# Layer norms of a two-layer hybrid decoder step: squares summed over features before the products, a short token block taken as a full one

## The chip, the cores and the metric

The kernel runs on one core of a Trainium2 chip. Its metric is the device time of one execution in microseconds (us), and the median of the runs counts. The engines are named as in the profile: PE is TensorE's matmul and PEld its weight loads, DVE is VectorE, ACT is ScalarE, POOL is GpSimd, SP issues most DMAs.

## What is computed

A prompt of 1024 tokens and 8 sample rows of 4 tokens go through two layers, together 1056 tokens of 1024 features. Each layer ends its two halves with a layer norm over the features:

```python
def layer_norm(x, g, b):
    xf = x.astype(jnp.float32)
    mu = jnp.mean(xf, -1, keepdims=True)
    var = jnp.mean(jnp.square(xf - mu), -1, keepdims=True)
    return ((xf - mu) * lax.rsqrt(var + LN_EPS)).astype(x.dtype) * g + b
...
    x = layer_norm(ALPHA * x + mix @ P['w_out'], P['ln1_g'], P['ln1_b'])
    h = jnp.square(jax.nn.relu(x @ P['w_ff_up']))
    x = layer_norm(ALPHA * x + h @ P['w_ff_down'], P['ln2_g'], P['ln2_b'])
```

The rest (RWKV-7 time mixing, windowed attention, gates) is untouched and is not told here.

## The kernel before

Activations lie feature-major: 8 feature tiles of 128 partitions, the tokens along the free dimension, in three chunks of 384, 384 and 288 tokens (`CH`). All large products are exact float32 products made of three float32r passes (`gemm_parts`): an output tile of one chunk takes 24 products for 1024 features, or 12 for a group of 512. Splitting a tile into its two parts (hi on ACT, lo on DVE or POOL) stands beside them.

There are 12 layer norms: two layers, two norms each (called the first and the second norm below), three chunks each. `layer_norm` is a generator with ten turns. Turn 1 issues the mean (one product of `ones`, which holds 1/1024, with the sum over the feature tiles that `add_up` has built on POOL, its last addition on DVE). Then, for each feature tile `k`, DVE subtracts the mean and ACT squares into a scratch tile `q`; in the turn after that PE multiplies the three 128-token blocks of `q` (the last block of the 288-token chunk has 32 tokens) with `ones[:, 0:32]`, which adds up the variance with the tokens on the partitions, in one PSUM tile `pv`. These are 24 products a norm. DVE then computes the reciprocal root in ten short steps on 128x3 elements (`newton`), spreads it into `ln_rb`, and in the last turn PE brings it back to the feature-major form with three products into `pr`. The rest of a norm is, per feature tile, one DVE multiplication by `pr`, one ACT pass for the bias, one ACT cast (hi) and one POOL subtraction (lo); the last norm of layer 1 has one ACT pass and a DMA to the output instead.

Two things set the order of the work. In the regions called `manual_schedule` PE's order is that of the program: `weave` issues the products of a projection one by one, and after each it takes the norm turns that are due by `book`, a list of times (`LN_TIMES`) on a count of PE time that the code keeps (`pe_ns`). So a norm's products sit between the products of the projection that comes after it. The other engines execute in an order that a scheduler makes from dependencies and program order; each engine runs its queue in order.

The first norm lies in `mix` and `ff`: `tail(c)` makes the last three tiles of the output projection for chunk `c` (72 products), books the norm of that chunk, and goes on with `tail(c+1)`; then come the up-projections of chunks 0, 1, 2 (72 products each), which need the normed chunk. The second norm lies at the end of `ff`: the last 96 products of the down-projection of each chunk, norms of chunks 0 and 1 booked, and the norm of chunk 2 issued after everything (`drain(norm(2))`). In layer 0 the next layer's projections follow on PE, in layer 1 the kernel ends.

Of the kernel before, what the change touches and what calls it, by code (L numbers as in the profile page):

```python
# [32 lines left out]
# z tiles in the order of the permuted w_in  # L33
# [4 lines left out]
# columns of the parameter table  # L38
# [10 lines left out]
# times of the tensor engine, ns: a slot of the chain, a unit of attention, what runs ahead of the first unit  # L49
SLOT, SLOTA, LEAD, LAG = 1790, 2720, 21000, 2  # L50
# slots of the products of each part, from the step's first (the first entry: what comes before its products)
# [17 lines left out]
# turns of a layer norm: the mean, the squares, the rest  # L69
LNT = [2200, 1800, 550, 2850]  # L70
LN_TIMES = [LNT[0]] + [LNT[0] + LNT[1] + LNT[2] * k for k in range(8)] + [LNT[0] + LNT[1] + 7 * LNT[2] + LNT[3]]


class Slots:
    """tiles of one token chunk in fixed places; the oldest freed place is taken next"""
# [24 lines left out]
class Step:  # L100
    """one pair of heads on one token chunk"""
# [10 lines left out]
class Kern:  # L112
# [47 lines left out]
    def load_consts(self):  # L160
# [3 lines left out]
        # scratch of the inverses: 32x32 blocks, zero but for their 16x16 blocks on the diagonal  # L164
# [5 lines left out]
    def load_x(self, pool, wts):  # L170
        """the input, split, by way of buffers that attention uses later, and the first weights"""
# [65 lines left out]
    def gemm_parts(self, w, k0, rhs, n):  # L237
        """gemm, with a stop after each product"""
# [12 lines left out]
    def gemms(self, parts):  # L251
        """gemms of generators, one after the other"""
        for p in parts:
            yield from p

    def split(self, src, hi, lo):
        """exact float32r parts of src"""
        self.nc.scalar.copy(hi, src)  # L258
        self.nc.vector.tensor_tensor(lo, src, hi.bitcast(F32), op=ALU.subtract)  # L259
# [4 lines left out]
    def newton(self, pool, v, shape, tag):  # L264
        """rsqrt of v > 0 (v is left as it is)"""
# [11 lines left out]
    def add_up(self, tmp, sums, acc, k, c):  # L277
        """the sum over the feature tiles, one tile more"""
# [7 lines left out]
    def layer_norm(self, tmp, small, acc, s, c, gcol, bcol, out=None):  # L286
        """ten turns: the mean, the squares of each feature tile, the rest"""
# [7 lines left out]
        # variance with the tokens on the partitions, rsqrt there, broadcast back  # L295
        blks = [(b, min(128, n - b)) for b in range(0, n, 128)]
        pv = self.ps(self.pb, "b")
        v = small.tile([128, 3], F32, tag="ln_v", name=self.nm("ln_v"))
        if n % 128:
            nc.gpsimd.memset(v, 1.0)  # L300
        for k in range(KD):
            nc.vector.tensor_tensor(a[k], a[k], pm[:, :n], op=ALU.subtract)
            q = get()
            nc.scalar.activation(out=q.f, in_=a[k], func=AF.Square)
            yield
            for bi in (0, 2, 1):
                b, m = blks[bi]
                self.mmul(pv[0:m, bi * 32:bi * 32 + 32], lhsT=q.f[:, b:b + m], rhs=self.ones[:, 0:32],
                                 start=(k == 0 and bi == 0), stop=(k == KD - 1 and bi == 1))
            q.put()  # L310
        nf = n // 128
        nc.vector.tensor_scalar(v[:, 0:nf], pv[:, 0:nf * 32:32], LN_EPS, None, op0=ALU.add)
        if n % 128:
            nc.vector.tensor_scalar(v[0:32, nf:nf + 1], pv[0:32, nf * 32:nf * 32 + 1], LN_EPS, None, op0=ALU.add)
# [5 lines left out]
        for bi, (b, m) in enumerate(blks):  # L320
            self.mmul(pr[:, b:b + m], lhsT=rb[0:m, bi, :], rhs=self.ident[0:m, 0:m], start=True, stop=True)
# [1230 lines left out]
```

## Time and profile before

| | us |
|---|---|
| median of 3 runs | 3635.3 |
| lowest and highest run | 3632.37 to 3644.65 |
| span of the profiled execution | 3640.7 |

The profiled execution has no separate time beside its span; the span lies 5.4 us above the median, inside the spread of the runs. TensorE is busy for 97% of the span and the chain of work that ended last lies on it for 85%. A page of this profile is read stage by stage: the granted clock (PEclk, 1.00 is 2.4 GHz and 0.50 is 1.2 GHz) is 1.00 nearly everywhere and lower in the slices that hold the layer norms, where PE also waits. In a timeline row, the first number is the start of the group, the second its length, xN the number of instructions; a float32 product is recorded as two instructions, so `x6` on `b<-ones,i` is one feature tile's three products. Matmuls overlap, so costs are taken from start to start.

### The profile page before, as it was taken

The page shows a single profiled execution, that of the slowest core. Times are in us where ns is not written, and L with a number is a line of the kernel's source. Part 1 is how long each engine was busy: PE and PEld are TensorE (multiplying, and loading weights), DVE is VectorE, ACT ScalarE, POOL GpSimd, SP SyncE. Part 2 cuts the span into 40 slices and gives each one's busy share as a digit, 9 for nine tenths or more (in the row PEclk, how much of TensorE's full clock was granted, in tenths as well). Part 3 has the DMA queues.
Part 4 walks back from the last instruction along what each step waited for, and adds up shares of the span by engine and source line. Part 5 has one row for each costly group of instructions (what it writes and reads, how often), then busy time and mean ns, then how long its engine had stood idle before and what let it go on. Part 6 is the DMA issues. An engine that isn't in the chain of part 4 may idle for free.

```text
span 3640.7 us, 64335 instructions
## 1 busy us (share of the span) xinstructions
PE 3547.2 (97%) x25646; PEld 3286.8 (90%) x25646; DVE 1954.5 (54%) x5190; ACT 1100.1 (30%) x2553; POOL 622.5 (17%) x988
## 2 busy tenths in 40 slices
PE   8999999998999999999999999999999999999998
PEld 8688888888989999999997888888799899999997
DVE  4646777756355333333547467777563443333335
ACT  4554322222142222222347443322221422222122
POOL 2223423210130000000242234222202200000001
PEclk9899999999989999999999999999899899999998
DMA  5133223225101111111031333222341111111111
GB/s 166 48 95 116 80 80 82 81 75 186 51 19 58 47 47 43 45 47 47 30 87 48 98 103 89 79 80 81 117 142 35 41 47 47 44 44 47 47 41 48
DMA packets 213228, 255.50 MB, mean 70 GB/s; under 512 B 103488, under 2 KB 175712, under 8 KB 212896
## 3 DMA queue, kind: packets, MB, share of 16 engines
q1 hardware_dynamic: 184032, 211.31, 19.9%
q10 hardware_dynamic: 27360, 35.57, 2.7%
q8 instruction: 202, 3.31, 0.4%
q0 software_dynamic: 1536, 4.52, 0.3%
q14 instruction: 98, 0.80, 0.1%
HBM read 188.99 MB, written 58.95 MB: 68 GB/s over the span
## 4 chain that ended last, share of the span: by engine, by line
PE 85%; DVE 3%; ACT 1%; issue 1%; POOL 1%; DMA 1%; SPq 0%; POOLq 0%; ACTq 0%; DVEq 0%
PE mm L203 44%; PE c L203 30%; PE b L203 9%; PE b L207 1%; POOL x L330 1%; PE c L207 0%; PE b L748 0%; DVE pd L974 0%; DMA i<-d_ya 0%; DMA i<-d_yr 0%; DVE Xt L976 0%; DVE A L1011 0%; ACT x L329 0%; DVE S L1092 0%; ACT x L328 0%
## 5 line engine op out<-in xcount | busy, mean ns | idle before, releaser
L203 PE MATMUL mm<-x,w 128*128 128x384 f32 (+1 forms) x7680 | 1452.3, 335 | 15.6 <-ACT x L258 6.9
L203 PEld LDWEIGHTS mm<-x,w 128*128 128x128 f32 x7680 | 1248.4, 191 | 70.0 <-issue 13.8
L203 PE MATMUL mm<-i,w 128*128 128x384 f32 (+1 forms) x3264 | 594.8, 325 | 17.2 <-ACT i L258 17.2
L203 PE MATMUL c<-i,w 128*128 128x384 f32 (+1 forms) x3264 | 589.1, 323 | 0.8 <-DVE i L1264 0.8
L203 PEld LDWEIGHTS mm<-i,w 128*128 128x128 f32 x3264 | 535.9, 189 | 20.9 <-ACT i L258 17.4
L203 PEld LDWEIGHTS c<-i,w 128*128 128x128 f32 x3264 | 533.8, 188 | 3.4 <-DVE i L1264 1.4
L224 ACT CAST w<-raw 128x1024 fp32r<-128x1024 f32 x232 | 243.3, 1049 | 756.5 <-PE c L203 546.1
L203 PE MATMUL c<-x,w 128*128 128x384 f32 (+1 forms) x2496 | 446.0, 326 | 0.0
L203 PEld LDWEIGHTS c<-x,w 128*128 128x128 f32 x2496 | 411.1, 190 | 0.4 <-DVE x L259 0.4
L225 DVE TENSOR_TENSOR w<-raw,w 128x1024 fp32r<-128x1024 f32 x232 | 287.0, 1237 | 100.9 <-ACT w L224 99.3
L1310 DVE TENSOR_TENSOR i<-i 128x384 f32<-128x384 f32 (+1 forms) x192 | 101.6, 530 | 366.1 <-ACT i L1309 366.1
L284 POOL TENSOR_TENSOR i<-i,i 128x384 f32<-128x384 f32 (+1 forms) x36 | 33.9, 941 | 1429.9 <-DVE i L1324 1425.9
L1324 DVE TENSOR_TENSOR i<-i,c 128x384 f32<-128x384 f32 (+1 forms) x168 | 87.4, 520 | 206.7 <-PE c L203 206.7
L1324 DVE TENSOR_TENSOR i<-i,mm 128x384 f32<-128x384 f32 (+1 forms) x168 | 87.0, 518 | 143.2 <-PE mm L203 143.1
L259 DVE TENSOR_TENSOR i<-i,i 128x384 fp32r<-128x384 f32 (+1 forms) x216 | 116.2, 542 | 72.9 <-ACT i L258 72.3
L258 ACT CAST i<-i 128x384 fp32r<-128x384 f32 (+1 forms) x216 | 104.6, 486 | 86.0 <-DVE i L1310 76.1
L776 POOL TENSOR_TENSOR z<-z,gs 128x384 f32<-128x384 f32 (+1 forms) x84 | 80.0, 953 | 290.8 <-issue 188.5
L1309 ACT ACTIVATE i<-c 128x384 f32<-128x384 f32 (+1 forms) x96 | 44.6, 465 | 231.0 <-PE c L203 231.0
L1309 ACT ACTIVATE i<-mm 128x384 f32<-128x384 f32 (+1 forms) x96 | 44.6, 465 | 210.7 <-PE mm L203 210.7
L1092 DVE SCALAR_TENSOR_TENSOR S<-c,eL,sd 64x64 f32<-64x64 f32 x256 | 72.4, 283 | 64.9 <-PE c L203 59.3
L1068 POOL TENSOR_SCALAR sd<-S,eL 128x128 f32<-128x128 f32 x128 | 96.7, 756 | 49.5 <-DVE S L1092 46.9
L1082 DVE COPY sav<-c 64x128 f32<-64x128 f32 x128 | 36.9, 288 | 126.1 <-PE c L203 125.0
(278 smaller groups left out, 4040.7 us busy)
## 6 DMA issues: line engine op xcount, KB each, us to landing
raw<-in_w_in_dram SPq DMA_DIRECT2D x72, 512.0 KB
raw<-in_w_up_dram SPq DMA_DIRECT2D x64, 512.0 KB
raw<-in_w_down_dram SPq DMA_DIRECT2D x64, 512.0 KB
d_g<-gs ACTq DMA_DIRECT2D x64, 192.0 KB
i<-d_g SPq DMA_DIRECT2D x64, 192.0 KB
d_z<-z ACTq DMA_DIRECT2D x52, 192.0 KB
raw<-in_w_out_dram SPq DMA_DIRECT2D x16, 512.0 KB
qrot<-qraw SPq DMA_DIRECT2D x40, 132.0 KB
```

The source lines that it names most:

```text
L203: return self.nc.tensor.matmul(out, lhsT=lhsT, rhs=rhs, start=start, stop=stop)
L224: nc.scalar.copy(wf[:, 0, :], raw)
L225: self.weng.tensor_tensor(wf[:, 1, :], raw, wf[:, 0, :].bitcast(F32), op=ALU.subtract)
L258: self.nc.scalar.copy(hi, src)
L259: self.nc.vector.tensor_tensor(lo, src, hi.bitcast(F32), op=ALU.subtract)
L776: nc.gpsimd.tensor_tensor(out[:, :n], out[:, :n], prev[:, :n], op=ALU.add)
L1068: nc.gpsimd.tensor_scalar(sd, S0, ecol, None, op0=ALU.mult)
L1082: nc.vector.tensor_copy(sav[B, :], sa[B, 0:128])
L1092: nc.vector.scalar_tensor_tensor(S1[r, r], pS[r, 0:64], ecol[r, :], sd[r, r], op0=ALU.mult, op1=ALU.add)
L1309: nc.scalar.activation(out=z.f, in_=p[:, :n], func=AF.Relu)
L1310: nc.vector.tensor_tensor(z.f, z.f, z.f, op=ALU.mult)
L1324: nc.vector.tensor_tensor(a, a, p[:, :n], op=ALU.add)
```

## The change

Per norm, except the two norms of chunk 2 at the end of a layer (`last=True`):

- The squares of feature tiles 0 and 1 are kept. Those of tiles 2, 4, 6 are added to the first on VectorE, those of 3, 5, 7 to the second on GpSimd. Then PE makes two times three products instead of eight times three.
- The ten turns become three, booked at 2200, 9400 and 13200 (before: 2200, eight from 4000 to 7850, and 10700).

The norm of chunk 2 of the second norm keeps its eight times three products, and issues each right behind its square, without turns. In all norms the third block of the 288-token chunk is taken as a full one that starts at token 160 and overlaps the second; the memset of `v` and the second, 32-row `tensor_scalar` fall away, and the broadcast back takes the last 32 columns of `ident` for that block.

```diff
-LNT = [2200, 1800, 550, 2850]
-LN_TIMES = [LNT[0]] + [LNT[0] + LNT[1] + LNT[2] * k for k in range(8)] + [LNT[0] + LNT[1] + 7 * LNT[2] + LNT[3]]
+LN_TIMES = [2200, 9400, 13200]
...
-        blks = [(b, min(128, n - b)) for b in range(0, n, 128)]
+        blks = (0, 128, n - 128)
         pv = self.ps(self.pb, "b")
         v = small.tile([128, 3], F32, tag="ln_v", name=self.nm("ln_v"))
-        if n % 128:
-            nc.gpsimd.memset(v, 1.0)
+
+        def var(q, first, final):
+            for bi, b in enumerate(blks):
+                self.mmul(pv[:, bi * 32:bi * 32 + 32], lhsT=q.f[:, b:b + 128], rhs=self.ones[:, 0:32],
+                          start=(first and bi == 0), stop=(final and bi == 2))
+            q.put()
+
+        sq = []
         for k in range(KD):
             nc.vector.tensor_tensor(a[k], a[k], pm[:, :n], op=ALU.subtract)
             q = get()
             nc.scalar.activation(out=q.f, in_=a[k], func=AF.Square)
+            if last:
+                var(q, k == 0, k == KD - 1)
+            elif k < 2:
+                sq.append(q)
+            else:
+                eng = (nc.vector, nc.gpsimd)[k % 2]
+                eng.tensor_tensor(sq[k % 2].f, sq[k % 2].f, q.f, op=ALU.add)
+                q.put()
+        if not last:
             yield
-            for bi in (0, 2, 1):
-                b, m = blks[bi]
-                self.mmul(pv[0:m, bi * 32:bi * 32 + 32], lhsT=q.f[:, b:b + m], rhs=self.ones[:, 0:32],
-                                 start=(k == 0 and bi == 0), stop=(k == KD - 1 and bi == 1))
-            q.put()
-        nf = n // 128
-        nc.vector.tensor_scalar(v[:, 0:nf], pv[:, 0:nf * 32:32], LN_EPS, None, op0=ALU.add)
-        if n % 128:
-            nc.vector.tensor_scalar(v[0:32, nf:nf + 1], pv[0:32, nf * 32:nf * 32 + 1], LN_EPS, None, op0=ALU.add)
+            var(sq[0], True, False)
+            var(sq[1], False, True)
+        nc.vector.tensor_scalar(v, pv[:, 0:96:32], LN_EPS, None, op0=ALU.add)
...
-        drain(norm(2))
+        drain(norm(2, last=True))
```

The first place is PE in the first norm of layer 0, around the squares of chunk 1. A row names the PSUM tile written, the two operands and the shape: `b_...<-ones,i` are the variance products, `b_...<-i,ones` is the mean, `ln_rb` the broadcast back, `c` and `mm` with `i` the output projection of chunk 2, `mm` with `x` the up-projection of chunk 0. Before, the variance products of chunk 1 start ten products after its mean, a set of three every third product:

```order
L203 MATMUL c_12212<-i_2_11_2215_11349,w_11916 128x288
L203 MATMUL b_12231<-i_1_6_2253_11626,ones 128x384
L203 MATMUL c_12212<-i_2_16_2229_11417,w_11916 128x288
L203 MATMUL c_12212<-i_2_2_2230_11418,w_11916 128x288
L203 MATMUL c_12212<-i_2_16_2229_11417,w_11916 128x288
```

Now two sets stand together, six products before the up-projection begins, 53 products behind the mean:

```order
L202 MATMUL c_12288<-i_2_15_2216_11350,w_11926 128x288
L202 MATMUL c_12288<-i_2_11_2215_11349,w_11926 128x288
L202 MATMUL b_12216<-ones,i_1_19_2318_12219 128x32 x3
L202 MATMUL b_12216<-ones,i_1_17_2319_12222 128x32 x3
L202 MATMUL c_12288<-i_2_16_2229_11417,w_11926 128x288
L202 MATMUL c_12288<-i_2_2_2230_11418,w_11926 128x288
```

The mean of chunk 2 and the broadcast of chunk 1 come next, after the first 14 and 15 products of the up-projection; the broadcast of chunk 1 used to stand ahead of that projection:

```order
L202 MATMUL mm_12351<-x_0_2308_12183,w_12338 128x384
L202 MATMUL b_12366<-i_2_6_2255_11654,ones 128x288
L202 MATMUL mm_12351<-x_14_2307_12182,w_12338 128x384
L202 MATMUL b_12401<-ident,ln_rb_12326 128x128 x3
L202 MATMUL mm_12351<-x_1_2309_12188,w_12338 128x384
```

What moved: the variance products of a chunk went from a stretch behind the mean to one point later, and the broadcasts later by some 15 products.

The second place is POOL in the first norm of layer 1 (layer 0 reads alike). `L341` is the lo part of a normed tile of chunk 0, `L283` the sum over feature tiles of chunk 2, `L318` the new additions of squares, of chunk 1 and of chunk 2. In the kernel before only `L341` (there L330) and `L283` (there L284) exist. Now:

```order
L341 TENSOR_TENSOR i_0_1_5460_30945<-x_11_5176_29194,x_10_5459_30944 128x384 [waits DMAHW5_49,PE_49,Activation_49]
L283 TENSOR_TENSOR i_2_6_5401_30398<-i_2_6_5401_30398,x_9_5190_29222 128x288 [waits DVE_49]
L283 TENSOR_TENSOR i_2_6_5401_30398<-i_2_6_5401_30398,x_10_5191_29224 128x288 [waits DVE_49,Pool_49]
L318 TENSOR_TENSOR i_1_17_5465_30966<-i_1_17_5465_30966,i_1_5_5467_30973 128x384 [waits Activation_49]
L318 TENSOR_TENSOR i_1_17_5465_30966<-i_1_17_5465_30966,i_1_10_5469_30981 128x384 [waits Activation_49,Pool_49]
L318 TENSOR_TENSOR i_1_17_5465_30966<-i_1_17_5465_30966,i_1_3_5471_30989 128x384 [waits Activation_49,Pool_49]
L318 TENSOR_TENSOR i_2_17_5488_31118<-i_2_17_5488_31118,i_2_5_5490_31125 128x288 [waits Activation_49]
```

What moved: the additions for chunk 1 stand behind all eight lo parts of chunk 0 and two sums of chunk 2.

The third place is PE at the start of layer 1, where the norm of chunk 2 of layer 0 lies among the next layer's projections (`mm` with `x`, of chunk 0). Before, its sets are spread:

```order
L203 MATMUL mm_19137<-x_9_3117_18599,w_18934 128x384
L203 MATMUL b_18944<-ones,i_2_11_3181_18948 128x32
L203 MATMUL b_18944<-ones,i_2_11_3181_18948 32x32
L203 MATMUL b_18944<-ones,i_2_11_3181_18948 128x32
L203 MATMUL mm_19137<-x_11_3119_18605,w_18934 128x384
```

Now the eight sets stand in a row, behind the 48th product of that layer:

```order
L202 MATMUL mm_19073<-x_4_3129_18606,w_18872 128x384
L202 MATMUL b_18882<-ones,i_2_11_3181_18885 128x32 x3
L202 MATMUL b_18882<-ones,i_2_15_3182_18891 128x32 x3
L202 MATMUL b_18882<-ones,i_2_1_3183_18897 128x32 x3
L202 MATMUL b_18882<-ones,i_2_12_3184_18903 128x32 x3
L202 MATMUL b_18882<-ones,i_2_16_3185_18909 128x32 x3
L202 MATMUL b_18882<-ones,i_2_2_3186_18915 128x32 x3
L202 MATMUL b_18882<-ones,i_2_13_3187_18921 128x32 x3
L202 MATMUL b_18882<-ones,i_2_14_3188_18927 128x32 x3
```

What moved: the first set was due 30 products into the new layer and had projections between it and the last; now no projection stands between the sets. The broadcast of chunk 1 went from the last stretch of the down-projection of chunk 2 to the 14th product of the new layer.

## Rows read from the trace of the kernel before

**Rows 1.** Busy time by stretch: engines, then granted clock, DMA share, GB/s.
```profile
997.62:1094.45 96.83, 88.32 (x529) 84.37 (x529) 49.89 (x116) 43.63 (x93) 27.54 (x29) 0.88 0.07 23
1767.51:1850.27 82.76, 74.45 (x436) 70.92 (x436) 46.49 (x109) 31.29 (x67) 29.59 (x33) 0.86 0.11 37
3566.86:3612.31 45.45, 43.61 (x305) 42.07 (x304) 28.70 (x70) 14.53 (x29) 9.30 (x11) 1.00 0.12 42
3612.31:3640.70 28.39, 12.77 (x58) 10.68 (x56) 11.68 (x36) 8.58 (x20) 1.58 (x2) 0.58 0.25 87
```

**Rows 2.** Timeline of PE, undisturbed projections: start us, length, group.
```profile
1505.27 2.24 PE L203 MATMUL mm<-i,w 128*128 128x384 f32 x12
1507.35 1.75 PE L203 MATMUL c<-i,w 128*128 128x288 f32 x12
1508.94 1.38 PE L203 MATMUL mm<-i,w 128*128 128x384 f32 x7
```

**Rows 3.** Timeline of PE, products of the norms of layer 0.
```profile
1000.05 0.81 PE L203 MATMUL b<-i,ones 128*128 128x384 f32 x2
1000.40 1.68 PE L203 MATMUL mm<-i,w 128*128 128x384 f32 x7
...
1013.27 0.85 PE L203 MATMUL b<-ident,ln_rb 128*128 128x128 f32 x6
1013.88 3.37 PE L203 MATMUL mm<-i,w 128*128 128x384 f32 x18
...
1023.92 0.75 PE L203 MATMUL b<-ones,i 128*128 128x32 f32 x6
1024.51 0.65 PE L203 MATMUL mm<-i,w 128*128 128x288 f32 x3
1024.99 0.75 PE L203 MATMUL b<-ones,i 128*128 128x32 f32 x6
```

**Rows 4.** Waits of PE from 985 to 1080: us, times, longest.
```profile
PE b L203 <- DVE i L284: 4.2, 2, 3.8
PE b L203 <- ACT i L304: 3.0, 2, 2.5
```

**Rows 5.** Timeline of ACT, first norm: from rest of chunk 0 to squares of chunk 1.
```profile
1014.89 0.62 ACT L328 ACTIVATE i<-i,par 128x384 f32<-128x384 f32 x1 [8.15 <-DVE i L323]
...
1023.81 0.51 ACT L329 CAST x<-x 128x384 fp32r<-128x384 f32 x1 [0.70 <-POOL x L330]
...
1026.42 1.35 ACT L304 ACTIVATE i<-x 128x384 f32<-128x384 f32 x3
```

**Rows 6.** Timeline of POOL, last lo part of chunk 0.
```profile
1024.50 1.00 POOL L330 TENSOR_TENSOR i<-x,x 128x384 fp32r<-128x384 f32 x1
```

**Rows 7.** Groups of POOL by shape: busy us, mean ns.
```profile
L284 POOL TENSOR_TENSOR i<-i,x 128x384 f32<-128x384 f32 x24 | 24.3, 1014 | 299.1 <-DVE x L1280 299.1
```

**Rows 8.** An addition elsewhere that DVE and POOL share: ns min/median/max.
```profile
L1249 DVE TENSOR_TENSOR x<-x,x x30: 444/544/1368, 827.4 to 2641.0; 128x384 f32<-128x384 f32 x20, 128x288 f32<-128x288 f32 x10
```

**Rows 9.** Timeline, second norm of layer 0: mean of chunk 1, rest of chunk 1.
```profile
1797.88 1.62 PE L203 MATMUL b<-i,ones 128*128 128x384 f32 x2 [3.13 <-DVE i L284]
...
1816.57 4.29 DVE L323 SCALAR_TENSOR_TENSOR i<-i,par,b 128x384 f32<-128x384 f32 x8 [1.80 <-PE b L203]
...
1819.36 4.94 POOL L330 TENSOR_TENSOR x<-i,x 128x384 fp32r<-128x384 f32 x4 [5.22 <-ACT x L329]
...
1824.31 0.91 ACT L329 CAST x<-i 128x384 fp32r<-128x384 f32 x2
```

**Rows 10.** Timeline of the kernel's end.
```profile
3609.27 4.29 DVE L323 SCALAR_TENSOR_TENSOR i<-i,par,b 128x384 f32<-128x384 f32 x8 [1.17 <-PE b L203]
...
3616.37 0.72 PE L203 MATMUL b<-i,ones 128*128 128x288 f32 x2 [3.90 <-DVE i L284]
3618.11 10.13 PE L203 MATMUL b<-ones,i 128*128 128x32 f32 x48 [1.02 <-ACT i L304]
```

**Rows 11.** Groups of PE by shape from 3617 to 3630: the 32-token blocks.
```profile
L203 PE MATMUL b<-ones,i 128*32 128x32 f32 x16 | 2.5, 252 | 0.0
```

More of the change, by code (lines that the diff above doesn't have):

```diff
@@ L284, in add_up, with layer_norm @@
             eng.tensor_tensor(sums[c].f, a, acc[k][c].f, op=ALU.add)
-    def layer_norm(self, tmp, small, acc, s, c, gcol, bcol, out=None):
+    def layer_norm(self, tmp, small, acc, s, c, gcol, bcol, out=None, last=False):
         nc, par = self.nc, self.par
@@ L319, in layer_norm @@
         pr = self.ps(self.pb, "b")
-        for bi, (b, m) in enumerate(blks):
-            self.mmul(pr[:, b:b + m], lhsT=rb[0:m, bi, :], rhs=self.ident[0:m, 0:m], start=True, stop=True)
+        for bi, b in enumerate(blks):
+            o, m = bi * 128, min(128, n - bi * 128)
+            self.mmul(pr[:, o:o + m], lhsT=rb[:, bi, :], rhs=self.ident[:, o - b:o - b + m], start=True, stop=True)
         for k in range(KD):
@@ L1361, in ff, with norm @@
         self.x = [[None] * 3 for _ in range(KD)]
-        def norm(c):
-            return self.layer_norm(inner, small, [acc[k][c] for k in range(KD)], sums[c], c, P_L2G, P_L2B,
+        def norm(c, last=False):
+            return self.layer_norm(inner, small, [acc[k][c] for k in range(KD)], sums[c], c, P_L2G, P_L2B, last=last,
                                    out=self.o["y"] if l == L - 1 else None)
```

## The prediction

> **What bounds the kernel now.** I read the stages that hold the norms first, as busy time by stretch [rows 1]. Stage A runs from the first product of chunk 1's tail to the end of nine up-projection units (96.8 us, first norm, layer 0; layer 1 has its like). Stage B is the end of layer 0, from chunk 1's last down-projections to the 72nd product of layer 1 (82.8 us). Stage C is the same in layer 1 as far as the last projection (45.5 us), stage D what follows to the end (28.4 us). In C TensorE is busy nearly throughout at full clock; in A and B the granted clock is 0.88 and 0.86, in D 0.58. So in A to C the tensor queue is the bound, with waits and a lower clock (1.2 instead of 2.4 GHz) on top; in D a chain through all engines is.
>
> Unit prices. Twelve products take 2.08 us at 384 columns and 1.59 at 288 [rows 2], 0.173 and 0.133 each. A set (one feature tile's three variance products) takes 0.59 start to start; three 288-column products between two sets take 0.48 instead of 0.40, so an interleaved set costs 0.67. A mean takes 0.35, a broadcast 0.61 [rows 3]. A norm therefore costs TensorE 8 x 0.67 + 0.96 = 6.3 us.
>
> Does that explain A? Projections: 216 products at 384 columns and 144 at 288, 56.5 us. Three norms: 19. Waits: 7.2 [rows 4]. Clock: 0.12 of 96.8, 11.6 [rows 1]. Sum 94.3 of 96.8. B: 41.8 + 19 + 11.6 for the clock, the rest waits.
>
> **The change, part by part.** *Products removed.* Ten norms lose six of eight sets; two sets that stand together cost 2 x 0.59 + 0.08 = 1.26. Each saves 8 x 0.67 - 1.26 = 4.1 us, a norm costs 2.2, and ten save 41 us at full clock. This is on the bounding queue, so it counts unless a wait takes its place. At the lower clock a set costs about twice, so where sets run there now (the third norm of A and of B) more is saved. I go through the stages because the booked turns decide the waits.
>
> *Stage A, after.* Count t from its start (997.62 in the trace). Mean of chunk 0 at 2.4, its two sets 40 products later at 9.7; subtractions, squares and additions need about 7 us from the mean (eight subtractions and three additions on VectorE, each like the 0.54 of [rows 8], and a POOL addition of 1.01 last [rows 7]), so they are just ready. Broadcast at 14.5, no wait. Its consequences are the point. Before, the broadcast at 1013.27 released ACT at 14.89, the eighth cast came at 23.81 (ACT waits there for POOL), and the last squares of the next chunk ended at 27.8, 14.5 after the broadcast [rows 3, 5]. The last lo part on POOL ended at 25.5, 12.2 after [rows 6]. After the change ACT's queue has the same order (less one weight cast), so the last square of chunk 1 comes at t = 14.5 + 14.5 = 29.0 at the latest. POOL has its lo parts until 26.7, then two sums of chunk 2 (0.8 each, three quarters of 1.01), then three new additions of 1.01 [rows 7]: 31.3. TensorE reaches the two sets of chunk 1 at 14.0 + 66 x 0.133 + 0.96 = 23.7. It waits until some 29 for the first, until 31.3 for the second, less a set between: **6.9 us of new wait**, and behind it on its queue stand the last six projections and the whole up-projection. Then VectorE: its Newton steps of chunk 1 share the queue with the first two subtractions of chunk 2, which need the mean of chunk 2, 14 products into the up-projection; the broadcast of chunk 1 stands one product behind that mean and waits for subtraction, Newton step, subtraction and copy, about 2.4. The last broadcast waits 0.5. Chunk 1's normed tiles are ready in time (12 us after their broadcast, needed 12 after). The wait before the mean of chunk 2 (3.8 now [rows 4]) goes, since VectorE's last sum now stands ahead of the multiplications.
> Clock: waits of 3.1 and 3.8 us [rows 4, 9] were followed by a lower clock now, so I charge a drop after each of the two larger waits: until projections have run some 3 us again, as at 1797.88 [rows 9]; half of that lost, 2.2 + 1.7. Total 56.5 + 3 x 2.2 + 9.8 + 3.9 = 76.8 against 96.8: **20 saved, twice: 40**.
>
> *Stage B, after.* Projections 41.8, transposes 0.3, two norms 4.4, and the third, whose eight sets stay, now in a row: 8 x 0.59 + 1.04 = 5.8. Waits: the mean of chunk 1 waits as now for POOL, which has four lo parts of chunk 0 (4.94) ahead of the sum [rows 9]: 3.6 instead of 3.1. The broadcast of chunk 1 comes at the 14th product of layer 1 and waits 0.6 for Newton steps behind the last sums. With E the last down-projection's end it is over at E + 3.6, VectorE's multiplications start at E + 4.2, and ACT's sixteen passes end 8.65 us after that start, as now (1816.57 to 1825.2 [rows 9]); only then come the squares of chunk 2, the first at E + 13.3. TensorE is at the first set after 48 products, at 8.3 + 0.6 + 0.96 = E + 9.9: 3.4 of wait. Eight sets in a row at the lower clock take 10.1 [rows 10] instead of 4.7, and some ten products after them twice their time: 5.4 + 1.7 lost, and 1.8 behind the mean of chunk 1. Total 52.3 + 7.6 + 8.9 = 68.8: **14 saved**.
>
> *Stage C, after.* 29.4 + 2 x 2.2 - 0.6 (a broadcast moves behind E) + 0.8 for the mean of chunk 1 = 34: **11.4 saved**.
>
> *Stage D, after.* The last sums no longer wait behind VectorE's multiplications of chunk 1 (3609.27 to 3613.6 [rows 10]), so the mean comes 2.2 earlier. But those 4.3 us now lie between E + 1.4 and E + 5.7, ahead of chunk 2's subtractions, and from the mean's end to the first set it takes 1.3 to 1.4 now (3616.7 to 3618.11): the first set at E + 7.0, now E + 5.8 [rows 10]. The clock is down by then, as now. The 24 products take 10.13 now [rows 10], of it 2.5 for the sixteen records of 32-token blocks [rows 11]; the other 32 take 7.6, so sixteen of full width 3.8: 1.3 more. **2.3 to 2.5 lost.** Elsewhere a full block in eight sets fewer is below what I can resolve; nobody waits for the memset in these stages [rows 4].
>
> Sum: -40 - 14 - 11.4 + 2.4 = **-63**. Against the profiled span 3640.7 that is 3578; against the median of 3635.3, which I predict, 3573 (rounded up).
>
> *What these costs hang on.* Additions on VectorE and GpSimd are not seen in the norm; an addition that both engines share elsewhere takes VectorE 0.54, at most 1.37 [rows 8], so bounds are 0.5 and 1.4. I take 0.5 to 0.6, as VectorE has slack before the sets of POOL are ready. The upper end on POOL too (three times 0.5 more) makes A 1.6 longer, twice.
> The Trainium skill, "SBUF — State Buffer", section "Who interferes with whom", says that a VectorE instruction with two SBUF inputs contends with a GpSimd instruction that reads SBUF, the loser being blocked for the whole instruction. Every new addition is of that kind and works against the change; the largest value of the row agrees with it. By the rule the gain would be 60 instead of 63.
>
> **The rivals.**
> *The clock holds* through the new waits. For it: 2.4 and 3.4 us are near the shortest wait that lowered it. A then saves 24 each, B 21, C 11, and D up to 4 (its sets at full clock): some 80 saved, 3555.
> *The waits are longer.* If additions on POOL meet VectorE's, if the squares of A come behind weight casts that wait for their DMA, or if the low clock lasts over the first up-projections (12.5 us of work, so 12 lost), A saves 8 to 12 each and B 10: 30 to 45 saved, 3598. For it: two sets in a row wait for the last of eight squares, where now a set waits for one square.
> *Slower.* The clock falls at the first new wait of A and stays at 1.2 GHz to the stage's end: 35 us of full-clock work behind it take 35 more, less the 3.9 charged, so A ends 11 over 96.8, both 22; with B saving 5 and C and D 9, that is 8 slower, 3643. It decides once the two stages lose 31 each on top, over 60 us of low clock a stage; now A has 0.12 x 96.8 x 2 = 23 in all [rows 1], with sets among its projections, of which few remain. Against it, strongly.
> *It doesn't do what it says:* the tensor queue only exchanges products for waits, all stages bound by the chain broadcast, ACT, POOL, square, addition. Then the time is that of now, 3635. Against it: C has 0.96 of its time in work at full clock [rows 1], and there 11 go whatever A does.
>
> **How the numbers follow.** Forecast (saving 50 to 75) 0.62; the clock holds 0.13; longer waits 0.20; no change 0.03; slower 0.02. A measurement of this kernel tells 0.3%, 11 us, from no change. Faster is the first three, 0.95. The range takes the forecast's bounds and most of both neighbours: from 78 saved (3557) to 37 (3598).
>
> **What would show it.** Right: 180 products of shape 128x32 fewer; C about 34 us long at clock 1.00; in A TensorE idle some 7 us for the two sets of chunk 1, released by POOL's addition, and about 2.4 for its broadcast; in B one wait for ACT's squares with eight sets in a row behind it, at 0.50; D about 31 us. Wrong: A near 73 with clock 1.00 (the first rival), A over 85 with long stretches at 0.50 (the second, or the slower case), C still 45, or a new wait in the up-projections for lo parts.

## The result, and the profile of the changed kernel

The changed kernel takes 3588.3 us (median of 4 runs, 3582.0 to 3594.4) against 3634.6 for the kernel before (4 runs): a ratio of 0.9868, 95% interval 0.9846 to 0.9890, so 40 to 56 us saved, about 48. In a second comparison (last experiment) the ratio was 0.9853, interval 0.9827 to 0.9879. Forecast were 63 saved and 3573 us: the sign and the range held, the forecast time was too low. The 48 saved lie between the 50 to 75 that the forecast had for itself and the 30 to 45 of its rival of longer waits; the 54 saved of the second comparison (0.0147 of 3642) lie within the first.

The profiled execution has a span of 3579.8 us, 60.9 less than the one of before. Not all of that is the change. Stage A begins at 987.34 instead of 997.62, and no layer norm stands ahead of it; in the ten later traces of this study it begins between 986 and 1003. I take those 10.3 us as scatter between executions. So I compare stages, in the windows that answer to [rows 1]. Columns: stretch, length, busy time (and instructions) of PE, PEld, DVE, ACT, POOL, then granted clock, DMA share, GB/s.

```profile
987.34:1070.37 83.03, 70.64 (x421) 69.04 (x421) 59.14 (x124) 43.42 (x93) 37.04 (x37) 0.92 0.09 26
1743.43:1811.34 67.91, 59.93 (x364) 57.95 (x364) 48.87 (x112) 30.02 (x65) 35.93 (x36) 0.92 0.14 45
3512.93:3549.68 36.75, 34.73 (x227) 33.38 (x226) 30.12 (x70) 12.24 (x24) 16.54 (x17) 1.00 0.12 43
3549.68:3579.80 30.12, 13.69 (x64) 12.71 (x62) 14.89 (x42) 10.66 (x24) 0.79 (x1) 0.55 0.26 92
```

A is 13.8 us shorter, B 14.9, C 8.7, D 1.7 longer; with A of layer 1 (14.1 shorter) that makes 50 saved, close to what the times say. PE in A is busy 17.7 us less, while VectorE has 9 us more to do and GpSimd 9.5: part of the products came back as waits. The waits of PE in A (columns: who waits and for whom, total, times, longest) answer to [rows 4], and the timeline shows where they stand:

```profile
PE b L202 <- DVE ln_rb L327: 6.1, 2, 4.7
PE b L202 <- DVE i L318: 4.7, 1, 4.7
PE b L202 <- POOL i L318: 1.6, 1, 1.6
```

```profile
997.34 1.42 PE L202 MATMUL b<-ones,i 128*128 128x32 f32 x12
...
1016.69 1.35 PE L202 MATMUL b<-ones,i 128*128 128x32 f32 x6 [4.68 <-DVE i L318]
1019.68 1.49 PE L202 MATMUL b<-ones,i 128*128 128x32 f32 x6 [1.64 <-POOL i L318]
...
1027.70 0.91 PE L202 MATMUL b<-ident,ln_rb 128*128 128x128 f32 x6 [1.36 <-DVE ln_rb L327]
...
1030.01 3.97 PE L202 MATMUL c<-x,w 128*128 128x384 f32 x22
...
1034.69 1.42 PE L202 MATMUL b<-ones,i 128*128 128x32 f32 x12
...
1044.58 1.46 PE L202 MATMUL b<-ident,ln_rb 128*128 128x128 f32 x6 [4.71 <-DVE ln_rb L327]
1045.86 6.44 PE L202 MATMUL c<-x,w 128*128 128x384 f32 x22
```

The first three waits were forecast: 6.9 us for the two sets of chunk 1 (measured 4.68 + 1.64), 2.4 for its broadcast (1.36). The last one was not: the broadcast of chunk 2 was given 0.5 us and took 4.71, and the 22 products behind it took 6.44 us where the same group elsewhere in A takes 3.97, because the clock was low (0.59 from 1045.86 to 1052.14, 1.00 in the group at 1030.01). VectorE's timeline says why the broadcast came late:

```profile
1021.48 1.22 DVE L224 TENSOR_TENSOR w<-raw,w 128x1024 fp32r<-128x1024 f32 x1
...
1034.69 7.33 POOL L341 TENSOR_TENSOR x<-x,x 128x384 fp32r<-128x384 f32 x6
...
1036.23 1.93 DVE L224 TENSOR_TENSOR w<-raw,w 128x1024 fp32r<-128x1024 f32 x1
...
1038.08 0.97 DVE L268 TENSOR_SCALAR ln<-ln_v 128x3 int32<-128x3 int32 x1
...
1039.09 0.92 DVE L270 TENSOR_TENSOR ln<-ln 128x3 f32<-128x3 f32 x1
...
1041.19 0.84 DVE L270 TENSOR_TENSOR ln<-ln 128x3 f32<-128x3 f32 x1
1042.07 0.16 DVE L271 SCALAR_TENSOR_TENSOR ln<-ln,ln_v 128x3 f32<-128x3 f32 x1
...
1042.64 0.99 POOL L341 TENSOR_TENSOR i<-x,x 128x384 fp32r<-128x384 f32 x1 [0.62 <-ACT x L340]
1042.66 0.99 DVE L271 SCALAR_TENSOR_TENSOR ln<-ln,ln_v 128x3 f32<-128x3 f32 x1
```

A Newton step works on three columns and takes 0.16 us. While GpSimd writes the low parts of chunk 1 (L341, six in a row until 1042.02), single steps take 0.84 to 0.97; the one that starts at 1041.19 ends at 1042.03, with GpSimd's sixth. The step at 1042.66 starts 0.02 after GpSimd's last low part and ends 0.02 after it. Five steps lose 3.8 us so, and the weight's low part ahead of them 0.7 (1.93 instead of 1.22 at 1021.48 in the same trace). In the kernel before, the same ten steps of chunk 2 come 16 us later in the stage, with GpSimd idle, and none of them takes longer than 0.17:

```profile
1064.46 0.17 DVE L269 TENSOR_SCALAR ln<-ln_v 128x3 int32<-128x3 int32 x1
1064.66 0.16 DVE L271 TENSOR_TENSOR ln<-ln 128x3 f32<-128x3 f32 x1
```

Elsewhere it is met too: of the 120 Newton steps in the trace, 26 take over 0.2 us, each of them beside GpSimd; in the kernel before, 7 of 120 do.

That reading became theory T2; that the gain is products less waits for sums is T1.

### The profile page after: what moved, and what is told of

It reads as the page before. It is cut to its first block, busy times and chain, and to the rows that moved or that the text cites. A ratio compares the mean times of both kernels' runs of the same rounds, so it can differ in the third digit from the quotient of the medians.

```text
span 3579.8 us, 63696 instructions
## 1 busy us (share of the span) xinstructions
PE 3476.0 (97%) x25286; PEld 3226.5 (90%) x25286; DVE 1980.9 (55%) x5216; ACT 1100.0 (31%) x2553; POOL 655.7 (18%) x1014
## 4 chain that ended last, share of the span: by engine, by line
PE 84%; DVE 5%; issue 1%; POOL 1%; ACT 1%; DMA 1%; SPq 0%; ACTq 0%; DVEq 0%; POOLq 0%
PE mm L202 44%; PE c L202 30%; PE b L202 8%; PE b L206 1%; DMA i<-d_ya 0%; PE c L206 0%; PE b L759 0%; DVE pd L985 0%; DVE Xt L987 0%; DVE x L1260 0%; POOL x L341 0%; DMA i<-d_yr 0%; DVE ln L270 0%; DVE ln L271 0%; DVE A L1022 0%
## 5 line engine op out<-in xcount | busy, mean ns | idle before, releaser
L202 PE MATMUL mm<-i,w 128*128 128x384 f32 (+1 forms) x3264 | 584.9, 323 | 17.4 <-ACT i L257 17.4
L224 DVE TENSOR_TENSOR w<-raw,w 128x1024 fp32r<-128x1024 f32 x232 | 287.1, 1237 | 98.0 <-ACT w L223 96.3
L283 POOL TENSOR_TENSOR i<-i,i 128x384 f32<-128x384 f32 (+1 forms) x36 | 36.4, 1012 | 1377.1 <-DVE i L1335 1372.9
L1093 DVE COPY sav<-c 64x128 f32<-64x128 f32 x128 | 36.8, 288 | 125.3 <-PE c L202 124.3
L1079 POOL TENSOR_SCALAR sd<-S,eL 128x128 f32<-128x128 f32 x128 | 96.8, 757 | 49.2 <-DVE S L1103 46.2
```

Source lines behind the costliest of these rows:

```text
L202: return self.nc.tensor.matmul(out, lhsT=lhsT, rhs=rhs, start=start, stop=stop)
L224: self.weng.tensor_tensor(wf[:, 1, :], raw, wf[:, 0, :].bitcast(F32), op=ALU.subtract)
L1079: nc.gpsimd.tensor_scalar(sd, S0, ecol, None, op0=ALU.mult)
L1093: nc.vector.tensor_copy(sav[B, :], sa[B, 0:128])
```

## The experiments

For each kernel below I give the ratio to the kernel before with its 95% interval, and the stages, each from the same product to the same product (so up to 0.3 us off the windows above). Single times scatter by some 8 us around their median, and the changed kernel came to 0.987 and 0.985 in two comparisons. A stage is read from one execution; in the two kernels that were profiled twice (e9, e10) it came within 1.2 us again, but one stage of e1 came out 5 us longer at a lower clock. Where a few microseconds matter I go by the stages, with that in mind. Times and lengths in us:

| kernel | time, ratio to before | A, layer 0 | A, layer 1 | B | C | D | sum |
|---|---|---|---|---|---|---|---|
| before | 3634.6 | 96.6 | 96.8 | 82.7 | 45.5 | 28.4 | 350 |
| changed | 3588.3, 0.987 | 83.0 | 82.7 | 68.0 | 36.8 | 30.1 | 301 |
| e1 block alone | 3636.0, 1.000 | 96.8 | 101.8 | 82.4 | 45.5 | 28.3 | 355 |
| e2 eight sets | 3618.5, 0.995 | 87.5 | 92.1 | 74.5 | 51.0 | 30.0 | 335 |
| e8 four sets | 3586.7, 0.987 | 84.0 | 84.6 | 69.4 | 38.4 | 29.1 | 306 |
| e3 Newton in PSUM | 3581.0, 0.984 | 78.1 | 79.3 | 70.7 | 35.2 | 29.2 | 293 |
| e4 sums on VectorE | 3593.8, 0.988 | 82.8 | 85.3 | 71.7 | 38.7 | 29.7 | 308 |
| e6 later turns | 3594.0, 0.988 | 84.8 | 82.6 | 71.1 | 34.6 | 34.5 | 308 |
| e5 last norms too | 3581.4, 0.986 | 82.0 | 83.3 | 67.3 | 36.6 | 26.3 | 296 |
| e7 Newton and last | 3572.2, 0.984 | 79.2 | 79.0 | 66.3 | 34.9 | 25.5 | 285 |
| e9 changed again | 3579.7, 0.985 | 83.0 | 81.5 | 68.2 | 36.8 | 30.1 | 300 |
| e10 e7 again | 3568.8, 0.981 | 78.8 | 78.8 | 65.7 | 35.2 | 25.2 | 284 |

**The full block alone.** The kernel before with only the block rule of the change (the lines that follow from it are left out):

```diff
-        blks = [(b, min(128, n - b)) for b in range(0, n, 128)]
+        blks = (0, 128, n - 128)
...
```

> The kernel before with the full third block alone: three sums of 128 tokens from one VectorE step, all eight squares still multiplied, ten turns as before. Theory T1 (the gain is products taken away, less new waits for additions): the number of products stays, so the time stays within 6 us of the kernel before and the layer norm's stage A stays at 95 to 98 us (96.8 before). Rival R1 (the block of 32 tokens costs by itself, in its odd-sized products and its second VectorE step): the time falls by 10 us or more, and A by 3 us or more.

Measured: 1.0003, interval 0.9983 to 1.0024. A is 96.8 in layer 0, B, C and D are those of before. A of layer 1 is 101.8, outside what I expected, at a granted clock of 0.80 (before 0.86) with about the same work and no more waits of PE (6.4 us, before 7.8). Layer 0 does not show it, so I take it for scatter of the clock, which one trace can't prove. R1 falls: the block costs and brings nothing beyond the interval, some 6 us less to 9 more.

**Turns without additions.** Three turns as in the changed kernel, all eight squares kept and multiplied in a row:

```diff
...
-            var(sq[0], True, False)
-            var(sq[1], False, True)
+            for k in range(KD):
+                var(sq[k], k == 0, k == KD - 1)
```

> The changed kernel without the additions: three turns as in the changed kernel, and at the second turn all eight squares are multiplied, 24 products in a row. T1: six sets of three products come back for each booked norm, at 0.59 us a set 3.5 us; three norms in each of two stages A (21 us), two in B (7 us), one or two in C (3.5 to 7 us), less what was waited for the additions (1.6 us of GpSimd and up to 4.7 us of VectorE in each A): 18 to 32 us slower than the changed kernel, A at 88 to 93 us against 83.0. Rival R2 (the three turns in one piece, not the fewer products, give the gain): within 8 us of the changed kernel, A below 86 us.

Measured: 0.9947 (0.9929 to 0.9966), 30 us above the changed kernel, inside T1's 18 to 32 and far from R2's 8; A is 87.5, just under T1's 88, and 92.1. But it is also faster than the kernel before, at the same number of products: by the stages (350, 335, 301) 15 of the 49 us come with the turns alone and 34 with the products taken away. So R2 has a third of the gain, and T1 the rest. The gain of the turns is in A and B. Before, the eight sets of A's chunk 2 were spread among the first up-projections, and that whole stretch of the kernel before ran at the low clock (0.50 in the column behind POOL's):

```profile
1047.00:1066.00 19.00, 17.79 (x73) 16.77 (x74) 2.63 (x12) 4.14 (x11) 1.26 (x2) 0.50 0.00 1
```

In one piece they run later and wait for no square. PE's waits in A fall from 8.5 us to 3.0, in B from 8.3 to 4.1. The list of A is first the row that [rows 4] leaves out for the kernel before (1.3 of the 8.5), then the only one with eight sets in a row:

```profile
PE b L203 <- DVE ln_rb L317: 1.3, 1, 1.3
```

```profile
PE b L202 <- DVE i L283: 3.0, 1, 3.0
```

C shows the other side. It has no wait before its sets, and still it is 5.5 us longer than before:

```profile
3550.68 1.20 PE L202 MATMUL mm<-i,w 128*128 128x384 f32 x6
3551.72 6.59 PE L202 MATMUL b<-ones,i 128*128 128x32 f32 x48
3558.12 2.27 PE L202 MATMUL mm<-i,w 128*128 128x384 f32 x6
```

These are start, length and group of PE in C. The 24 products (48 records) take 6.4 us instead of 5.3 as at 1003.70 in A of the same trace (the last section has that row), and the six projections behind them 2.07 start to start instead of 1.04. PE was not idle there, before the row or within it, and yet the granted clock fell (0.87 in C, 1.00 before). Of the eleven rows of 24 products in this trace that no wait stands right before, ten met the lower clock, within the row or right behind it; one, at 1764.48 in B, did not. The rows of 6 and 12 products in the changed kernel and with four sets, where no wait stood before them, met none. So the additions also keep the single piece short.

**Four sets.** One size changed: four sums of two squares.

```diff
-            elif k < 2:
+            elif k < 4:
...
-                eng.tensor_tensor(sq[k % 2].f, sq[k % 2].f, q.f, op=ALU.add)
+                eng.tensor_tensor(sq[k % 4].f, sq[k % 4].f, q.f, op=ALU.add)
...
```

> The changed kernel with half of the additions: four sums of two squares each and four sets at the second turn. T1 (products taken away count one by one): two more sets for each of the ten norms, less the two done without additions, so eight norms by 2 x 0.59 us, 9.4 us, less 0.5 to 1.0 us of additions in each: 4 to 9 us slower than the changed kernel; A at 84 to 86 us. Rival R7 (the waits for the sums, not the sets, are the price, and shorter chains of additions give them back): the time within 3 us of the changed kernel or below it, the wait before the sets of chunk 1 in A under 4 us.

Measured: 0.9868 (0.9842 to 0.9893), equal to the changed kernel in total, which is what R7 said of the time; T1 had 4 to 9 us more. In the stages it is 5 us more, as T1 has it (A 1.0 and 1.9 longer, B 1.4, C 1.6; D 1.0 shorter), a difference that the times can't resolve. PE in A:

```profile
1015.23 1.49 PE L202 MATMUL b<-ones,i 128*128 128x32 f32 x6 [3.24 <-DVE i L318]
1017.15 4.05 PE L202 MATMUL b<-ones,i 128*128 128x32 f32 x18 [0.44 <-POOL i L318]
...
1045.23 0.86 PE L202 MATMUL b<-ident,ln_rb 128*128 128x128 f32 x6 [3.55 <-DVE ln_rb L327]
```

The wait before the sets of chunk 1 is 3.2 + 0.4 instead of 6.3, under 4 as R7 has it, and the last broadcast waits 3.55 instead of 4.71. Still A is no shorter: the six additional sets take it back, and chunk 1's run at the low clock, 1.3 us each. T1 against R7 stays undecided here. Between two and four sets little is to be had; eight cost 30 us.

**Newton in PSUM.** The running estimate of the layer norms moves to a free part of the variance bank, so that each step reads at most one operand from SBUF:

```diff
-        r = self.newton(small, v, (128, 3), "ln")
+        r = self.newton(small, v, (128, 3), "ln", y=pv[:, 128:131])
...
-            nc.vector.tensor_tensor(u, y, y, op=ALU.mult)
-            nc.vector.scalar_tensor_tensor(u, u, -0.5, v, op0=ALU.mult, op1=ALU.mult)
+            nc.vector.tensor_tensor(u, y, v, op=ALU.mult)
+            nc.vector.scalar_tensor_tensor(u, u, -0.5, y, op0=ALU.mult, op1=ALU.mult)
```

> The changed kernel with the Newton estimate of the layer norms kept in PSUM, so that no step of it reads two operands from SBUF; the order of the steps is the same, y*y*v is computed as (y*v)*y. Theory T2 (the 4.71 us wait for the last broadcast in A comes from Newton steps of VectorE that stand still while GpSimd writes the low parts, because both read two operands from SBUF): the steps of chunk 2 go back to 0.15 to 0.3 us each, the wait in A falls to below 1.5 us, and the low clock behind it goes with it: A falls by 3 to 6 us (83.0 to 77 to 80), the time by 6 to 12 us. Rival R3 (the wait comes from the queue ahead of the steps: the weight's low part on VectorE between the variance and the first step): the steps stay at 0.8 to 1.0 us or the wait stays above 3 us, A changes by less than 1.5 us.

Measured: 0.9835 (0.9803 to 0.9866), 0.2 to 0.3% below the changed kernel, which the totals alone would not settle; A 78.1 and 79.3 instead of 83.0 and 82.7. The first lines below are from the list of the lines' instructions in the changed kernel (count: shortest, median and longest in ns, first and last start), the next the same steps with the estimate in PSUM (left out: the steps of L271 and L272):

```profile
L268 DVE TENSOR_SCALAR ln<-ln_v x12: 168/483/975, 999.0 to 3567.9; 128x3 int32<-128x3 int32 x12
...
L270 DVE TENSOR_TENSOR ln<-ln x36: 151/161/921, 999.6 to 3569.3; 128x3 f32<-128x3 f32 x36
```

```profile
L268 DVE TENSOR_SCALAR b<-ln_v x12: 147/164/166, 1003.6 to 3567.0; 128x3 int32<-128x3 int32 x12
...
L270 DVE TENSOR_TENSOR ln<-b,ln_v x36: 146/160/161, 1003.8 to 3568.4; 128x3 f32<-128x3 f32 x36
```

None of the 120 steps is longer than 0.17 us now, though 61 of them overlap work of GpSimd, those of chunk 2 the same low parts. The timeline of chunk 2 in that kernel:

```profile
1036.73 1.85 DVE L224 TENSOR_TENSOR w<-raw,w 128x1024 fp32r<-128x1024 f32 x1
...
1043.02 5.23 POOL L341 TENSOR_TENSOR x<-x,x 128x384 fp32r<-128x384 f32 x5 [0.40 <-ACT x L340]
...
1044.75 0.16 DVE L270 TENSOR_TENSOR ln<-b,ln_v 128x3 f32<-128x3 f32 x1
...
1047.30 0.75 PE L202 MATMUL b<-ident,ln_rb 128*128 128x128 f32 x6
1047.89 4.08 PE L202 MATMUL c<-x,w 128*128 128x384 f32 x22
```

The broadcast waits for nothing and the 22 products behind it take 4.08 us at full clock, not 6.44. That the steps stood still for GpSimd, and no longer do, is shown. The wait of 4.71 is not theirs alone: the edit also changed VectorE's order, and the weight's low part (L224) that stood between the variance and the first step, R3's cause, now runs long ahead of both (1036.73, the variance step at 1044.37). The steps had lost 3.8 us and the low part took 1.9; this run does not separate them. So T2 has the larger part and R3 falls as the main cause, but not as a share. The shorter A is no scatter: in the three kernels with the estimate in PSUM it is 78.1 to 79.3 in all six readings, in the changed kernel's two traces and with the last norms by additions 81.5 to 83.3. In C the same edit takes away the wait of 1.35 us before the first broadcast (36.8 to 35.2). Two things run against it: the steps of chunk 1 in A now stand between five subtractions on VectorE instead of two, so that broadcast waits 3.52 instead of 1.36; and in B, where the broadcast comes earlier, the wait passes to the last norm's sets (3.89 for ScalarE instead of 2.17, then 10.45 us for the sets instead of 8.22): 2.7 us longer.

The Trainium skill ("SBUF — State Buffer", section "Who interferes with whom") says that VectorE and GpSimd share a pair of ports under an exclusive lock, that a VectorE instruction with two SBUF inputs contends with a GpSimd instruction that reads SBUF, and that a `tensor_scalar` can contend too when its operands meet certain conditions. The rows agree: steps of both kinds stand still until GpSimd's instruction ends (0.84 to 0.99 us instead of 0.16), and with the estimate in PSUM neither kind does (0.17 at most).

**All sums on VectorE.**

```diff
-                eng = (nc.vector, nc.gpsimd)[k % 2]
+                eng = nc.vector
```

> The changed kernel with all six additions on VectorE, none on GpSimd. T1 (VectorE and GpSimd share the additions so that the last of them ends about 1.6 us after VectorE's own): GpSimd's wait of 1.6 us before the second set goes, and three more additions of 0.45 to 0.6 us stand in VectorE's row, between the next subtractions and the weights' low parts: A within 2 us of 83.0, the time within 6 us of the changed kernel. Rival R4 (GpSimd's additions, 0.9 to 1.2 us each, and what they hold up on VectorE are what the layer norm waits for): A falls by 3 us or more, the time by 8 us or more. A third way, VectorE's queue becomes the bound: A rises by 3 us or more.

Measured: 0.9879 (0.9844 to 0.9915), A 82.8 and 85.3: what T1 allows, in layer 1 a little more, and no fall as R4 has it. The sets of chunk 1 wait 5.6 us in one piece instead of 6.3 in two:

```profile
1020.21 2.77 PE L202 MATMUL b<-ones,i 128*128 128x32 f32 x12 [5.63 <-DVE i L318]
```

This row is PE's timeline at that place. B and C are 3.7 and 1.9 us longer than in the changed kernel, which I did not trace further. Sharing the sums with GpSimd is no loss that these runs could show.

**Later turns.** The sets and the broadcast of a booked norm come later in the tensor queue, so that runnable up-projections stand ahead of them:

```diff
-LN_TIMES = [2200, 9400, 13200]
+LN_TIMES = [2200, 13000, 16500]
```

> The changed kernel with the second and third turn of each booked norm 3.6 and 3.3 us of products later, so that the two sets of chunk 1 in A stand behind the first up-projections of chunk 0, which can run. Theory T3 (the 6.3 us before these sets are a matter of the tensor queue's order): the waits before the sets fall below 3 us and A falls by 3 to 6 us (83.0 to 77 to 80). Rival R5 (the chain broadcast, ScalarE, low parts on GpSimd, squares, sums sets the stage): the wait comes back before the broadcast of chunk 1, or in the up-projections of chunk 1, whose low parts come later: A within 2 us of 83.0 or longer.

Measured: 0.9884 (0.9856 to 0.9912); A 84.8 and 82.6. PE's waits in A:

```profile
PE b L202 <- DVE ln_rb L327: 8.5, 2, 7.1
PE mm L202 <- POOL x L341: 3.1, 5, 1.1
PE mm L202 <- ACT x L340: 1.2, 1, 1.2
```

No wait is left before the sets of chunk 1. It stands now before the broadcast of chunk 1 (7.1 us) and in the first up-projection, product by product behind GpSimd's low parts. The waits of A sum to 12.8 us (12.4 in the changed kernel). T3 falls, R5 holds: the 6.3 us belong to the chain broadcast, ScalarE, low parts, squares, sums, and this other place in the queue only moves them. Outside A it moves work too: C is 2.2 us shorter and D 4.4 longer, since in layer 1 the sets and the broadcast of the second norm's chunk 1 now stand behind all projections, the broadcast with 3.15 us of wait.

**The last norms too.** The last norm of each layer, which the change leaves with eight sets, by additions:

```diff
-        drain(norm(2, last=True))
+        drain(norm(2))
```

> The changed kernel with the last chunk's second norm of each layer also by additions, so that its eight sets (8.22 us in B and 10.45 us in D, both at the low clock) become two. T1 (a set taken away gains its time, less the wait for the sums): two sets at the low clock take 2.1 to 2.6 us, and the sums end 1.5 to 2.5 us after the last square: 4 to 6 us less in B (68.0 to 62 to 64), 5 to 7 us less in D (30.1 to 23 to 25), the time 9 to 13 us less. Rival R6 (the chain of squares and sums sets these two places and the products lie beside it): B and D change by less than 2 us each, the time by less than 4.

Measured: 0.9855 (0.9831 to 0.9879), 0.1 to 0.2% below the changed kernel in total, 7 us by the medians where 9 to 13 were expected; D 26.3 instead of 30.1, B 67.3 instead of 68.0. First D's sets in the changed kernel, then here:

```profile
3557.24 10.45 PE L202 MATMUL b<-ones,i 128*128 128x32 f32 x48 [4.68 <-ACT i L311]
```

```profile
3569.31 2.77 PE L202 MATMUL b<-ones,i 128*128 128x32 f32 x12 [8.20 <-DVE i L318]
```

The sets give back 7.7 us and the wait before them grows by 3.5, more than the 1.5 to 2.5 that I had put: the sums alternate with the subtractions on VectorE, and ScalarE's squares wait for these (0.5 before the last two). In B the wait grows by 3.9 (2.17 to 6.03) against 5.4 of sets. T1 holds in kind for D, with the sums underpriced; in B R6 holds.

**Both edits, and both kernels once more.** Newton in PSUM with the last norms by additions; then this and the changed kernel together, in five rounds.

> Both edits together: the Newton estimate in PSUM, and the last norm of each layer by additions. If T2 and T1 hold and their gains add up, A is at 78 to 79 us and D at 23 to 25 us, and the time is 14 to 20 us below the changed kernel, 3568 to 3574. If R6 holds for the last norm, the time is that of the kernel with Newton in PSUM alone, 3576 to 3584.

> The changed kernel as it is, once more, on the chip and in the rounds of the next run: 46 to 50 us below the kernel before, 3585 to 3590 us if the kernel before is at 3635; A at 82 to 84 us in both layers, the last broadcast of A waiting 4.7 us, if that wait belongs to the program and not to one execution.

> The kernel with both edits (Newton estimate in PSUM, last norms by additions), once more, beside the changed kernel. From the stages of the first runs (A 4 us less in each layer, B and C 2 each, D 4 to 5) it should stand 14 to 18 us below the changed kernel, an interval that does not touch it. If the first runs differed by chance, within 6 us of it.

Measured: 0.9836 (0.9809 to 0.9864) first, at 3572 us, with A at 79 and D at 25.5. By the stages the two gains add up (285, against 293 and 296 with one edit each and 301 with none); the ratio, no lower than the 0.9835 of Newton in PSUM alone, doesn't show it. Then 0.9814 (0.9788 to 0.9839) with the changed kernel at 0.9853 beside it. In the last comparison each of the six times of the combined kernel (3563 to 3573 us) is below each of the six of the changed one (3579 to 3593); medians 11 us apart, stages 16. The intervals of the two ratios still overlap by a little, so the size, 11 to 16 us where I had put 14 to 18, is less sure than the order. The changed kernel is 62 us below the kernel before by these medians, 54 by the ratio, more than I had put (46 to 50). The last broadcast of its A waited 4.71 us again, so this belongs to the program (A 83.0, and 81.5 in layer 1, just under what I had put). The combined kernel is the fastest of this study, 60 to 68 us below the kernel before by its two ratios.

## Why the prediction came out as it did

*What bounds the kernel, and the sum.* Right in the mechanism. The gain is products taken off the bounding queue, less new waits: 180 products went (360 records), the full block costs nothing that can be measured (e1), and the four stages hold the whole difference. 50 us were saved in the stages of 63 forecast. By e2, 15 of them come with the three turns alone, at the same number of products; the forecast counted one wait that goes with the turns (3.8 us in A) and did not set this share apart.

*Stage A* is the step that was off in size: 76.8 forecast, 83.0 measured, 82.7 in layer 1: 12 of the 13 us that are missing, with the other stages nearly even. Products at full clock (56.5) and norms (3 x 2.2) stand as put. The waits were 9.8 forecast and are 12.4 (4.68 + 1.64 + 1.36 + 4.71); the rest, 7.5 us, is by my estimate mostly the clock (a mean of 0.92 over 83 us leaves 6.6), forecast 3.9. The mis-sized term is the last broadcast, 0.5 us forecast, 4.71 measured, and the low clock behind it, which the forecast charged after two waits and not after a third. With Newton in PSUM, and the weight's low part ahead, that wait and the low clock behind it go, and A comes to 78.1 and 79.3. I had weighed such blocking for the new additions alone and taken it as 3 us. There the forecast was good: VectorE's additions of squares have a median of 0.55 us. But the change also brings chunk 2's Newton steps under chunk 1's low parts, where before they had GpSimd idle beside them, and tiny steps pay up to a whole GpSimd instruction each. (The readings of the kernel before were a little off too: its waits were 8.5 us in A, not 7.2, and 8.3 in B, not the 10.4 that the sum leaves.)

*Stage B.* 68.8 forecast, 67.9 measured, but that is luck: errors cancel. The mean of chunk 1 waits 2.70 (3.6 forecast), ScalarE's squares 2.17 (3.4), the eight sets 8.2 (10.1): each smaller. Against these stand 2.9 for two broadcasts, 0.6 forecast.

*Stage C.* 34 forecast, 36.75 measured. 1.35 of it is the wait for the first broadcast, again a Newton estimate beside GpSimd's additions; e3 removes it. It was 0.79 before and I had left it out. The mean of chunk 1 waits 0.65 (0.8 forecast). The remaining 1.5 us lie in small gaps that I did not trace.

*Stage D.* 2.4 longer forecast, 1.7 measured, again with some luck: the first set comes 1.8 us later (7.56 into the stage, before 5.80; 1.2 forecast), while the eight sets take 10.45 us, 0.3 more than in [rows 10], where 1.3 more were forecast for the full blocks. In e1 they take 10.45 too, and D is 28.3.

*The rivals.* The clock did not hold (0.92 in A and B); the stage that never falls into low clock is C. The forecast called waits of 2.4 and 3.4 us near the shortest that had lowered it, but in B of the kernel before a wait of 2.18 was followed by the low clock already (0.50 from 1814.91 to 1818.20), twelve projections taking 2.33 us start to start instead of 1.59:

```profile
1814.91 1.62 PE L203 MATMUL b<-ident,ln_rb 128*128 128x128 f32 x6 [2.18 <-DVE ln_rb L317]
...
1816.57 2.49 PE L203 MATMUL mm<-i,w 128*128 128x288 f32 x12
1818.90 1.75 PE L203 MATMUL c<-i,w 128*128 128x288 f32 x12
```

Longer waits is the rival that came closest: it had 8 to 12 saved in A and 10 in B, the forecast 20 and 14; measured are 13.8 and 14.9, so A came nearer to the rival and B to the forecast. The cause in A was another, though. That additions on GpSimd are the price was wrong (e4). That the chain only exchanges products for waits is wrong for the whole and right for one place: the 6.3 us before the sets of chunk 1 can't be moved away (e6). What the prediction lacked is that a row of 24 products can cost clock without waiting (e2): with two sets instead of eight in that row, C is 14.2 us shorter, twice the 7.1 of twelve sets at 0.59.

## What to carry to other kernels

When additions replace products, ask which short steps the new order sets beside the other engine's long instructions: a chain of ten steps on three columns is cheap alone, and costs up to a whole GpSimd instruction at each step that meets one. Keep such a chain's running value in PSUM, or its place clear of GpSimd. And before moving a wait in a queue, follow what releases it: if that is a chain through three other engines, the wait comes back at the next place which needs its end.

## What the runs showed of the hardware

- A VectorE step of 0.16 us (128x3, SBUF operands) takes 0.84 to 0.99 beside GpSimd's `tensor_tensor` of 128x384 (1.0 us alone) and ends within 0.03 us behind it; with the estimate in PSUM it keeps 0.16. The step with one SBUF input (L268) does so as well: 0.97, and 0.17 when it writes PSUM.
- Rows of 24 products of 32 columns, without a wait right ahead of them or within them, met the lower granted clock in ten cases of eleven: 15 projections behind such a row took 4.25 us start to start (2.6 at full clock), six took 2.07 (1.04). In the eleventh, at 1764.48, the granted clock stayed at 1.00 and six projections took 1.13. What sets that one apart is open.

```profile
1003.70 5.44 PE L202 MATMUL b<-ones,i 128*128 128x32 f32 x48
1008.98 4.41 PE L202 MATMUL mm<-i,w 128*128 128x384 f32 x15
1013.23 0.83 PE L202 MATMUL b<-ident,ln_rb 128*128 128x128 f32 x6
...
1764.48 5.44 PE L202 MATMUL b<-ones,i 128*128 128x32 f32 x48
1769.76 1.29 PE L202 MATMUL mm<-i,w 128*128 128x384 f32 x6
1770.89 1.73 PE L202 MATMUL c<-i,w 128*128 128x384 f32 x9
```

These rows are PE's timeline in A and in B of the kernel with eight sets in a row. The six products of two sets, also in one piece, were not followed by it: at 997.34 in the changed kernel, 18 projections behind them took 3.20.
